# Two gate products computed while x arrives, earlier evacuation of two value tiles, and fewer buffers held back at the end of gate and up

## The chip, the cores and the metric

The kernel runs on one core of a Trainium2 chip. The metric is device time in microseconds (us) of one execution. The kernel before takes 737.2 us (median of 3 runs, 736.91 to 737.78). One more execution was profiled: it took 737.0 us, of which 735.2 us are the span that the profile shows.

A core has five engines that each run their own list of instructions strictly in order and wait for each other by semaphores: PE (matrix multiplications; PEld is its loading of weights), DVE (VectorE), ACT (ScalarE), POOL (GpSimd) and SP (which here only issues transfers). Transfers run on 16 DMA engines beside them. Matrix products go to PSUM, eight banks of 128 x 512 float32; everything else lies in SBUF.

## The reference

One encoder layer on x of 512 tokens by 1024 features, in float32:

```
proj = h @ w_in                              # queries, keys and values of two mixers
o_a = windowed_gqa_sink(qa, ka, va, sink)    # mixer A: 16 heads, 4 key heads
o_b = dilated_mixture(qb, kb, vb)            # mixer B: 12 heads in 3 groups
gates = sigmoid(h @ w_gate + b_gate)
mixed = g_a * (o_a @ w_br_a) + g_b * (o_b @ w_br_b)
h = layer_norm(ALPHA * h + mixed @ w_out)
f = (silu(h @ w_ff_gate) * (h @ w_ff_up)) @ w_ff_down
h = layer_norm(ALPHA * h + f)
```

## The kernel before

**Products.** Each float32 operand is split into two parts, a rounded high part (a copy, mostly on ACT, line 357) and the rest as a low part (a subtraction on DVE, lines 383, 406 and 469). A product of 128 x 128 weights with 512 columns of x is three matmuls (lines 496 to 498: high by high, high by low, low by high). A *unit* is 128 output features by all 1024 inputs: eight such steps of k, three matmuls each, into one PSUM bank. Its weights come in two halves of 256 KB (`half_unit`), each of which takes a landing buffer ("ws") and two buffers for its parts ("whl").

**The start.** x lies in memory as eight tiles xT of 128 features by 512 tokens (256 KB). Three units are computed along with its arrival, one each of keys, queries and values: for k = 0 to 7 the three matmuls of each (lines 1025 to 1035). Their first weight halves come in three pieces (`CUTS`: 128, 128 and 256 columns). After them follow two gate units ("g2", the first word of `ORDER`), then the second value unit ("VA"), and so on. A gate unit ends with a tanh on ACT (line 1007) that reads its PSUM bank.

**Values.** `turned_values` computes two value units, copies each from PSUM to SBUF on ACT (`evac`, printed as line 357), turns them by transposes on PE (line 681) and splits them again.

**Gate and up.** 22 times, `quad` computes 128 features of the gate and the up product by seven products of half size (12 matmuls of 256 columns each, lines 1422 to 1424), which share two PSUM banks y and xz. What stands in a bank is copied out by ACT (`keep`, line 357) before the next product may be added in the same place. The sums for the down product (`Chunk`) are worked in between; pieces for them are rounded by ACT at line 1610.

**Who sets the order.** Nothing waits by hand. The program is written as a list of operations with priorities, and a planner (`Program.run`) plays it through while the kernel is built, with a cost for every operation: at each moment a free engine takes the ready operation of highest priority whose buffers fit. What comes out is a fixed list for each engine. The priority is a point of PE's time, moved by a constant: `EV = -100` for what empties PSUM, `NORM = -150`, -130 for weights (`LOOK`); the smaller goes first. The operations at the start have absolute places (`FIRST`). `limits` says how many buffers of a class may be in use at a time, and `spare` how many of the general ones only the oldest waiting operation may take.

Of the kernel before, what the change touches and what calls it, by code (L numbers as in the profile page):

```python
# [15 lines left out]
P = 128  # L16
S = 512
# [48 lines left out]
         ("k", 1): (-996.9,), ("q", 1): (-996.7,), ("v", 1): (-996.6,),  # L66
         "x": (-999, -998.75, -997.5, -996.95, -996.8, -996.5, -996.4, -996.3)}
X_PACE = {1: None}
N_WS, N_WHL, N_ATT = 6, 12, 16


# [5 lines left out]


ORDER = """
g2 VA q1 A0 q2 q3 A1 g k1 q4 g q5 A2 g q6 g q7 A3 g2  # L80
Q00 K00 Q01 K01 V12 Q02 K02 V0 B0 Q10 K10 B1 Q11 K11 Q12 K12 B2 B3 g8
"""

# [34 lines left out]
class Program:  # L118
# [67 lines left out]
    def run(self):  # L186
# [26 lines left out]
        while n_left:  # L213
            if not times:
                self.stuck(pending)
            now = heapq.heappop(times)
            while times and times[0] <= now:
                heapq.heappop(times)
            while frees and frees[0][0] <= now:
                _, _, b = heapq.heappop(frees)  # L220
                for key in b.keys:
                    if key in self.limits:
                        self.used[key] -= 1
            progress = True
            while progress:
                progress = False
                for e in engines:
                    if free[e] > now:
                        continue
                    best = None  # L230
                    soon = now
                    for o in pending[e]:
                        if o.hold and now < o.ready <= now + HOLD and e in (DVE, ACT):
                            soon = o.ready
                        if o.ready <= now and (best is None or o.prio < best.prio) and self.fits(o):
                            if e == DVE and len(o.alts) > 1 and free[ACT] < now + BIAS:
                                continue
                            best = o
                    if best is None or soon > now and not best.hold:
                        continue  # L240
                    o = best
                    cost = dict(o.alts)[e]
                    if e == ACT and o.table not in (None, table):
                        cost, table = cost + 1.28, o.table
                    for a, _ in o.alts:
                        pending[a].remove(o)
                    for b in o.bufs:
                        if b.tile is None:
                            b.tile = b.make()
                            for key in b.keys:  # L250
                                if key in self.limits:
                                    self.used[key] += 1
                    o.fn(e)
                    o.eng = e
                    if e == SP:
                        end = now + 0.47
                        moved = max(moved, now + 0.9) + (1.5 if now < 5 else 0.92) * cost
                        o.done = moved + 0.87
                    elif o.moves:
                        end = now + cost  # L260
# [55 lines left out]
def hybrid_layer(ctx: ExitStack, tc: tile.TileContext, wpack, xT, xtok, sink, bgate,  # L316
# [6 lines left out]

    N_SLOT, HP = 85, S // 2
    pr = Program({"slot": N_SLOT, "bank": 8, **BANKS,
                  "ws": N_WS, "whl": N_WHL, "att": N_ATT, "gen": N_SLOT - 2 - N_ATT - N_WS - N_WHL,
                  "unit": UNITS, "st": 4, "x4": 4, "wf": N_WF})
    op = pr.op
    mm = nc.tensor.matmul
# [44 lines left out]
    def cp_alts(n, ps=False, cut=0.0):  # L374
        return [(ACT, act(n, ps) + cut), (DVE, dve(n, not ps) + cut)]
# [74 lines left out]

    first = {}
    for j in range(2):
        for w, u in (("k", U_KA), ("q", U_QA), ("v", U_VA)):
            first[w, j] = half_unit_by(u, j, ((0, S),) if j else CUTS, FIRST[w, j])
    got = {}
    for j in range(KD):
        st, ap = slot(F32, "xs"), FIRST["x"][j]
# [48 lines left out]
    def feat_x(ps, wu):  # L506
        for k in range(KD):
            feat_k(ps, wu, k, XM, xtok_of)
# [143 lines left out]
    def turned_values(u, nt, turn_by=0, done=None):  # L652
# [3 lines left out]
        for i in range(2):  # L656
# [13 lines left out]
                    else:  # L670
                        copy(e, d, s)

            op(cp_alts(S, True, 0.3 if turn_by else 0.1)[:2 if turn_by else 1], evac, reads=[ps], writes=[t], prio=EV)
            src.append(t)
        res = []
        for b in range(NR):
# [322 lines left out]

    away = {}  # L1000

    def gate(f, put=False):
        ps = bank("dense")
        feat_x(ps, unit(U_GATE + f))
        t = slot()
        gz[f] = t
        op([(ACT, act(S, True, 1))], lambda e: nc.scalar.activation(
            halves(t.t), back(ps.t), AF.Tanh, bias=bg.t[:, f:f + 1], scale=0.5),
           reads=[ps, bg], writes=[t], prio=EV)
        if put:  # L1010
            d = Buf("dram", None, lambda: dram.tile([P, S], F32, name=name("gz")))
            op([(SP, 0.73)], lambda e: nc.sync.dma_start(d.t, t.t), reads=[t], writes=[d], prio=EV)
            away[f] = d

    def dense_q(u, nt, kv_half):
        ps = bank("dense")
# [6 lines left out]
        return k_post(ps, nt) if nt else k_pairs(ps)  # L1023

    psk, psq, psv = bank("dense"), bank("dense"), bank("dense")
    for k in range(KD):
        for w, ps in (("k", psk), ("q", psq), ("v", psv)):
            for c in (0, S // 2) if (w, k) == ("k", 0) else (None,):
                if c is None:
                    feat_k(ps, [first[w, 0], first[w, 1]], k, XM, xtok_of, split=w == "k")  # L1030
                else:
                    op_ = feat_k(ps, [first[w, 0], first[w, 1]], k, XM, lambda k, c=c: [(xh4[0], 0, c), (xl4[0], 0, c)],
                                 n0=c, n1=c + S // 2, begins=c == 0, split=True)
                    if c == 0:
                        fill(op_)
    ka = k_near(psk, 4)
    qa = q_near(psq, 4, (0, 0))
    load(mB, maskb, prio=0)
    env = {"gate": 0, "qs": {}, "ks": {}}

    def step(w):
        if w == "VA":
# [10 lines left out]
                unit_a(g, b, qa[4 * g:4 * g + 4], ka[g], env["va"])  # L1053
        elif w[0] in "gG":
            for _ in range(int(w[1:] or 1)):
                gate((env["gate"] + 8) % 16, w[0] == "G")
                env["gate"] += 1
        elif w[0] in "QK":
            pair, g = int(w[1]), int(w[2])
# [610 lines left out]
            out[t, :, j * S + c0:j * S + c1], xt[t, j].t[:, c0:c1]), reads=[tok])  # L1670

    op([(POOL, 0.0)], lambda e: pr.limits.update(whl=4 * (N_LAST + 2)), after=[silus[-2]])
    n0 = 2 * N_PAIR * N_CHUNK
    tok_major(NFF - n0, N_LAST, lambda k: su[n0 + k], U_DOWN + n0, lg2, lb2, store, True, 1.0,
              lambda t: [chunks[c].step(n) for c, n in STEPS.get(("block", t), ())], (2, 3))
# [101 lines left out]
```

## Time and profile before

| what | us |
|---|---|
| median of 3 runs | 737.2 |
| the profiled execution | 737.0 |
| its span | 735.2 |
| PE busy in the span | 725.2 |
| DVE busy | 653.7 |
| ACT busy | 447.4 |
| POOL busy | 109.5 |

The engines' shares are averages over stages that differ. Busy PE means that a matmul is under way; since matmuls overlap, the distance from one start to the next tells whether PE lost time between them. In a row of the timeline stand the start, the duration, the engine, the line, the operation and the tiles; in brackets how long the engine was idle just before and what released it.

### The profile page before, as it was taken

The page shows a single profiled execution, that of the slowest core. Times are in us where ns is not written, and L with a number is a line of the kernel's source. Part 1 is how long each engine was busy: PE and PEld are TensorE (multiplying, and loading weights), DVE is VectorE, ACT ScalarE, POOL GpSimd, SP SyncE. Part 2 cuts the span into 40 slices and gives each one's busy share as a digit, 9 for nine tenths or more (in the row PEclk, how much of TensorE's full clock was granted, in tenths as well). Part 3 has the DMA queues.
Part 4 walks back from the last instruction along what each step waited for, and adds up shares of the span by engine and source line. Part 5 has one row for each costly group of instructions (what it writes and reads, how often), then busy time and mean ns, then how long its engine had stood idle before and what let it go on. Part 6 is the DMA issues. An engine that isn't in the chain of part 4 may idle for free.

```text
span 735.2 us, 13431 instructions
## 1 busy us (share of the span) xinstructions
PE 725.2 (99%) x4479; PEld 663.0 (90%) x4479; DVE 653.7 (89%) x1428; ACT 447.4 (61%) x1012; POOL 109.5 (15%) x273
## 2 busy tenths in 40 slices
PE   9999999999999999999999999999999999999995
PEld 6888888888888889888888999999999999999985
DVE  5879998898898999897686999799999999899977
ACT  5647687757665657774352567656666556666721
POOL 0000110000003323500010002111102111202100
PEclk9999999999999999999999999999999999999999
DMA  8824523437234765455583389776888978978402
GB/s 270 289 58 144 163 82 87 129 94 204 76 93 138 201 176 163 137 170 174 165 205 88 86 250 233 178 179 154 203 254 195 221 196 237 243 196 180 112 29 86
DMA packets 69252, 120.17 MB, mean 163 GB/s; under 512 B 8576, under 2 KB 12800, under 8 KB 69184
## 3 DMA queue, kind: packets, MB, share of 16 engines
q1 hardware_dynamic: 59040, 101.10, 44.7%
q0 software_dynamic: 9872, 18.09, 15.2%
q8 instruction: 35, 0.57, 0.3%
q14 instruction: 33, 0.27, 0.1%
q10 hardware_dynamic: 272, 0.13, 0.1%
HBM read 103.04 MB, written 2.10 MB: 143 GB/s over the span
## 4 chain that ended last, share of the span: by engine, by line
PE 94%; DMA 2%; DVE 2%; SPq 1%; ACT 1%; issue 0%; DVEq 0%; ACTq 0%
PE ps L497 12%; PE ps L496 12%; PE ps L498 12%; PE ps L1422 9%; PE ps L1424 9%; PE ps L1423 9%; PE ps L1633 4%; PE ps L1635 4%; PE ps L1634 4%; PE ps L749 3%; PE ps L1192 3%; PE ps L1193 3%; PE ps L1194 3%; PE ps L647 1%; PE ps L646 1%; PE ps L815 1%
## 5 line engine op out<-in xcount | busy, mean ns | idle before, releaser
L357 ACT ACTIVATE sl<-sl 128x512 fp32r<-128x512 f32 (+3 forms) x383 | 210.6, 582 | 62.0 <-DVE sl L1312 17.3
L1312 DVE TENSOR_TENSOR sl<-sl,sl 128x512 fp32r<-128x512 f32 (+3 forms) x294 | 167.1, 609 | 6.2 <-ACT sl L357 3.4
L357 ACT ACTIVATE sl<-ps 128x256 f32<-128x256 f32 (+5 forms) x205 | 85.8, 441 | 99.7 <-PE ps L1424 60.1
L496 PE MATMUL ps<-x,sl 128*128 128x512 f32 (+1 forms) x369 | 142.4, 386 | 0.3 <-ACT x L357 0.3
L498 PE MATMUL ps<-x,sl 128*128 128x512 f32 (+1 forms) x369 | 139.8, 379 | 0.0
L497 PE MATMUL ps<-x,sl 128*128 128x512 f32 (+1 forms) x337 | 127.9, 379 | 0.2 <-DVE x L469 0.2
L1422 PE MATMUL ps<-sl,sl 128*128 128x256 f32 x352 | 96.9, 275 | 0.6 <-ACT sl L357 0.6
L1423 PE MATMUL ps<-sl,sl 128*128 128x256 f32 x352 | 96.8, 275 | 0.0
L1424 PE MATMUL ps<-sl,sl 128*128 128x256 f32 x352 | 96.8, 275 | 0.0
L383 DVE TENSOR_TENSOR sl<-sl,sl 128x512 fp32r<-128x512 f32 x130 | 87.2, 685 | 5.1 <-ACT sl L357 4.5
L498 PEld LDWEIGHTS ps<-x,sl 128*128 128x128 f32 x369 | 69.9, 189 | 9.9 <-DVE sl L406 0.2
L496 PEld LDWEIGHTS ps<-x,sl 128*128 128x128 f32 x369 | 70.2, 190 | 8.7 <-ACT x L357 0.5
L371 POOL DMA_DIRECT2D sl<-wpack x44 | 38.5, 883 | 260.3 <-DMA sl<-wpack 72.7
L1422 PE MATMUL ps<-x,sl 128*128 128x256 f32 x264 | 72.6, 275 | 0.0
L1423 PE MATMUL ps<-x,sl 128*128 128x256 f32 x264 | 72.6, 275 | 0.0
L1424 PE MATMUL ps<-x,sl 128*128 128x256 f32 x264 | 72.6, 275 | 0.0
L497 PEld LDWEIGHTS ps<-x,sl 128*128 128x128 f32 x337 | 64.0, 190 | 7.5 <-DVE x L469 0.5
L1422 PEld LDWEIGHTS ps<-sl,sl 128*128 128x128 f32 x352 | 67.6, 192 | 0.8 <-ACT sl L357 0.7
L1423 PEld LDWEIGHTS ps<-sl,sl 128*128 128x128 f32 x352 | 67.6, 192 | 0.1
L1424 PEld LDWEIGHTS ps<-sl,sl 128*128 128x128 f32 x352 | 67.6, 192 | 0.0
L1422 PEld LDWEIGHTS ps<-x,sl 128*128 128x128 f32 x264 | 50.6, 192 | 0.4
L1423 PEld LDWEIGHTS ps<-x,sl 128*128 128x128 f32 x264 | 50.6, 192 | 0.4
(151 smaller groups left out, 1547.1 us busy)
## 6 DMA issues: line engine op xcount, KB each, us to landing
sl<-wpack SPq DMA_DIRECT2D x243, 256.0 KB, 3.7
sl<-sl SPq DMA_DIRECT2D x108, 128.0 KB, 2.3
wf<-wpack SPq DMA_DIRECT2D x51, 256.0 KB, 5.0
sl<-wpack POOLq DMA_DIRECT2D x44, 256.0 KB, 5.9
wf<-wpack POOLq DMA_DIRECT2D x24, 256.0 KB, 6.3
sl<-xtok SPq DMA_DIRECT2D x8, 256.0 KB, 3.3
out<-sl SPq DMA_DIRECT2D x7, 256.0 KB, 2.0
sl<-xT SPq DMA_DIRECT2D x6, 256.0 KB, 5.6
```

The costliest lines, as they stand in the source:

```text
L357: nc.scalar.activation(dst, src, AF.Copy)
L371: op([(POOL, 1.0)], lambda e: nc.gpsimd.dma_start(b.t, src2, accum_op=ALU.add), reads=[b], writes=[b], prio=prio, moves=1.65)
L383: op([(DVE, dve(S))], lambda e: nc.vector.tensor_tensor(l.t, src.t, f32(h.t), op=ALU.subtract), reads=[src, h], writes=[l], prio=prio, abs ...
L496: mm(o, a, x0, start=(k == 0 and begins), stop=False, skip_group_check=split)
L497: mm(o, a, x1, start=False, stop=False, skip_group_check=split)
L498: mm(o, b, x0, start=False, stop=(k == nk - 1), skip_group_check=split)
L1312: op([(DVE, dve(w))], lambda e: nc.vector.tensor_tensor(dst(), x(), y(), op=o), reads=reads, writes=writes, prio=prio)
L1422: mm(o, wh, pairs(bh[k]()), start=(first and k == 0), stop=False, skip_group_check=True)
L1423: mm(o, wh, pairs(bl[k]()), start=False, stop=False, skip_group_check=True)
L1424: mm(o, wl, pairs(bh[k]()), start=False, stop=(k == 3), skip_group_check=True)
L1633: mm(ps.t, x0, pairs(w[0].t), start=(first and m == 0), stop=False, skip_group_check=True)
L1634: mm(ps.t, x0, pairs(w[1].t), start=False, stop=False, skip_group_check=True)
```

## The change

Two gate units (features 8 and 9) are computed along with x: at each step of k there are now five products (keys, queries, values and the two gates). Their banks come from the class "s" (the two banks that later hold scores), their first halves are loaded in two pieces of 256 columns (128 KB, `ALONG_CUTS`), and "g2" goes from the head of `ORDER`. While this runs, 24 instead of 12 buffers for weight parts and two more landing buffers may be in use. The copy of the value units out of PSUM gets priority `NORM` instead of `EV`. From the third last silu on, `spare` is 8 instead of 12. The planner's costs change too: DVE's operations count 3% longer in the first 60 us, a transfer's issue counts 0.62 instead of 0.47 us between 14 and 60 us, and its data come more slowly in the first 9.5 us (before: 5 us) and 1.53 us later between 9.5 and 60 us. The unused `put` of `gate` is removed.

PE has the same number of matmuls as before. In the stretch that ran from about 365 to 664 us of the profiled span the lists of all engines are the same as before but for tiles' numbers; they differ ahead of it (the start, the two mixers, and the loads around the output product) and behind it (the last tiles of gate and up).

In the rows below each name carries the tile's number; wpack is the packed weights, xT the tiles of x.

SP's list at the start, before (sl3, sl5 and sl6 receive the weights of keys, queries and values; the row of xT with sl17 is the fourth tile of x, k = 3):

```order
L464 DMA sl8_98<-xT 128x512
L402 DMA sl3_75<-wpack 128x256
L402 DMA sl5_83<-wpack 128x256
L402 DMA sl6_85<-wpack 128x256
L464 DMA sl17_131<-xT 128x512
L402 DMA sl19_138<-wpack 128x512
L464 DMA sl21_147<-xT 128x512
```

and now (sl12 and sl15 receive the gates' weights, sl23 the fourth tile of x):

```order
L467 DMA sl8_98<-xT 128x512
L405 DMA sl12_105<-wpack 128x256
L405 DMA sl15_113<-wpack 128x256
L405 DMA sl3_75<-wpack 128x256
L405 DMA sl5_83<-wpack 128x256
L405 DMA sl6_85<-wpack 128x256
L405 DMA sl12_105<-wpack 128x256
L405 DMA sl15_113<-wpack 128x256
L467 DMA sl23_157<-xT 128x512
L405 DMA sl26_166<-wpack 128x512
L467 DMA sl27_169<-xT 128x512
```

The fourth tile of x moves back by four pieces of 128 KB; everything ahead of it stays.

ACT's list around the copies of the two value units, before (ps86 is the bank of the second one, that of the first stands two rows ahead of this piece; rows at line 1007 are the tanh of gates; 64x512 rows are parts of rotated keys and queries):

```order
L357 ACTIVATE sl73_363<-sl56_298 64x512 x2
L357 ACTIVATE sl77_374<-sl52_288 128x512
L1007 ACTIVATE sl79_382<-ps62_312,bg_67 128x512
L357 ACTIVATE sl74_364<-sl74_364 64x512
L357 ACTIVATE sl81_398<-sl53_293 128x512
L357 ACTIVATE sl84_406<-sl67_337 64x512
L357 ACTIVATE sl87_423<-sl64_320 128x512
L1007 ACTIVATE sl89_429<-ps76_369,bg_67 128x512
L357 ACTIVATE sl91_443<-sl65_326 128x512
L357 ACTIVATE sl95_462<-sl66_332 128x512
L357 ACTIVATE sl97_468<-ps86_419 128x4x64 x2
```

and now (ps20 and ps91 are the values, ps29 and ps31 the two gates):

```order
L360 ACTIVATE sl84_403<-sl67_348 128x512
L360 ACTIVATE sl86_409<-ps20_143 128x4x64 x2
L360 ACTIVATE sl88_418<-sl70_357 128x512
L360 ACTIVATE sl92_428<-sl73_366 128x512
L1011 ACTIVATE sl95_433<-ps29_180,bg_67 128x512
L1011 ACTIVATE sl96_439<-ps31_188,bg_67 128x512
L360 ACTIVATE sl100_465<-sl80_392 64x512 x2
L360 ACTIVATE sl102_472<-sl80_392 64x512
L360 ACTIVATE sl105_482<-ps91_424 128x4x64 x2
```

Both tanh now stand together, and the second value unit follows closely on the first, behind parts of the rotated keys.

ACT's list near the end of gate and up, before (ps1909 is the bank y of the last quad; its row is the copy that PE needs):

```order
L357 ACTIVATE sl1922_9044<-wf1818_8500 128x512
L357 ACTIVATE sl1924_9061<-sl1897_8881 128x512
L1610 ACTIVATE sl1927_9067<-sl1821_8519 128x256
L1610 ACTIVATE sl1928_9069<-sl1889_8851 128x256
L1610 ACTIVATE sl1929_9072<-sl1895_8874 128x256
L357 ACTIVATE sl1930_9074<-ps1909_8964 128x256
```

and now (the bank is ps1922):

```order
L360 ACTIVATE sl1930_9073<-sl1871_8777 128x512
L360 ACTIVATE sl1932_9078<-sl1901_8909 128x512
L1614 ACTIVATE sl1934_9094<-sl1894_8868 128x256
L360 ACTIVATE sl1935_9096<-sl1875_8797 128x512
L1614 ACTIVATE sl1937_9100<-sl1899_8891 128x256
L360 ACTIVATE sl1938_9103<-ps1922_9019 128x256
```

One of the three roundings at line 1610 has gone some 25 rows ahead, and a copy of a whole tile stands among them; the silu ahead of them also comes earlier.

```diff
+N_ALONG, N_WHL0 = 2, 24
+ALONG_CUTS = ((0, 256), (256, 512))
+FIRST.update({(0, 0): (-997.45, -996.97), (0, 1): (-996.65,), (1, 0): (-997.4, -996.96), (1, 1): (-996.45,)})
...
-g2 VA q1 A0 q2 q3 A1 g k1 q4 g q5 A2 g q6 g q7 A3 g2
+VA q1 A0 q2 q3 A1 g k1 q4 g q5 A2 g q6 g q7 A3 g2
...
-                    cost = dict(o.alts)[e]
+                    cost = dict(o.alts)[e] * (1.03 if e == DVE and now < 60 else 1.0)
...
-                        end = now + 0.47
-                        moved = max(moved, now + 0.9) + (1.5 if now < 5 else 0.92) * cost
-                        o.done = moved + 0.87
+                        end = now + (0.62 if 14 < now < 60 else 0.47)
+                        moved = max(moved, now + 0.9) + (1.5 if now < 9.5 else 0.92) * cost
+                        o.done = moved + (2.4 if 9.5 < now < 60 else 0.87)
...
-                  "ws": N_WS, "whl": N_WHL, "att": N_ATT, "gen": N_SLOT - 2 - N_ATT - N_WS - N_WHL,
+                  "ws": N_WS + 2, "whl": N_WHL0, "att": N_ATT, "gen": N_SLOT - 2 - N_ATT - N_WS - N_WHL,
...
-        for w, u in (("k", U_KA), ("q", U_QA), ("v", U_VA)):
-            first[w, j] = half_unit_by(u, j, ((0, S),) if j else CUTS, FIRST[w, j])
+        for w, u in (("k", U_KA), ("q", U_QA), ("v", U_VA), *((i, U_GATE + 8 + i) for i in range(N_ALONG))):
+            first[w, j] = half_unit_by(u, j, ((0, S),) if j else ALONG_CUTS if w in range(N_ALONG) else CUTS, FIRST[w, j])
...
-            op(cp_alts(S, True, 0.3 if turn_by else 0.1)[:2 if turn_by else 1], evac, reads=[ps], writes=[t], prio=EV)
+            op(cp_alts(S, True, 0.3 if turn_by else 0.1)[:2 if turn_by else 1], evac, reads=[ps], writes=[t], prio=NORM)
...
+    along = [bank("s") for _ in range(N_ALONG)]
     for k in range(KD):
-        for w, ps in (("k", psk), ("q", psq), ("v", psv)):
+        for w, ps in (("k", psk), ("q", psq), ("v", psv), *enumerate(along)):
...
+    op([(POOL, 0.0)], lambda e: pr.limits.update(whl=N_WHL, ws=N_WS), after=[pr.ops[-1]])
+    for f in range(N_ALONG):
+        gate(8 + f, along[f])
...
+    op([(POOL, 0.0)], lambda e: setattr(pr, 'spare', 8), after=[silus[-3]])
```

More of the change, by code (lines that the diff above doesn't have):

```diff
@@ L1000, in hybrid_layer, with gate @@
     away = {}
-    def gate(f, put=False):
-        ps = bank("dense")
-        feat_x(ps, unit(U_GATE + f))
+    def gate(f, ps=None):
+        if ps is None:
+            ps = bank("dense")
+            feat_x(ps, unit(U_GATE + f))
         t = slot()
@@ L1009, in gate @@
            reads=[ps, bg], writes=[t], prio=EV)
[L1010 to L1013, printed above, removed]
     def dense_q(u, nt, kv_half):
@@ L1038, in hybrid_layer @@
     load(mB, maskb, prio=0)
-    env = {"gate": 0, "qs": {}, "ks": {}}
+    env = {"gate": N_ALONG, "qs": {}, "ks": {}}
     def step(w):
@@ L1055, in step @@
             for _ in range(int(w[1:] or 1)):
-                gate((env["gate"] + 8) % 16, w[0] == "G")
+                gate((env["gate"] + 8) % 16)
                 env["gate"] += 1
```

## The prediction

> **What bounds the kernel now.** I read the page's busy times first, then who PE waited for, then the timeline at those places.
>
> ```profile
> span 735.2 us, 13431 instructions
> PE 725.2 (99%) x4479; PEld 663.0 (90%) x4479; DVE 653.7 (89%) x1428; ACT 447.4 (61%) x1012; POOL 109.5 (15%) x273
> ```
>
> PE is busy for 725.2 of 735.2 us. The change leaves the number of matmuls as it is, so it can only win what PE loses between them, and lose by new gaps. The list of waits of PE names all that it lost visibly:
>
> ```profile
> PE ps L433 <- DVE eps L483: 1.2, 1, 1.2
> PE ps L1422 <- ACT sl L357: 0.6, 1, 0.6
> PE ps L1192 <- DVE sl L1126: 0.4, 1, 0.4
> PE ps L496 <- ACT x L357: 0.3, 1, 0.3
> PE ps L497 <- DVE x L469: 0.2, 1, 0.2
> ```
>
> The first row is the very start, the last two are the arrival of a tile of x, L1422 is in gate and up, L1192 in the output product. The list counts only time with no matmul under way, so the full loss is read from the starts. PE at the tile of x:
>
> ```profile
> 10.60 0.38 PE L498 MATMUL ps<-x,sl 128*128 128x512 f32 x1
> 10.84 0.48 PE L496 MATMUL ps<-x,sl 128*128 128x512 f32 x1
> 11.16 0.38 PE L497 MATMUL ps<-x,sl 128*128 128x512 f32 x1
> 11.38 0.41 PE L498 MATMUL ps<-x,sl 128*128 128x512 f32 x1
> 12.04 0.48 PE L496 MATMUL ps<-x,sl 128*128 128x512 f32 x1 [0.25 <-ACT x L357]
> 12.76 0.48 PE L497 MATMUL ps<-x,sl 128*128 128x512 f32 x1 [0.24 <-DVE x L469]
> 13.08 0.38 PE L498 MATMUL ps<-x,sl 128*128 128x512 f32 x1
> ```
>
> Undisturbed, such matmuls start 0.216 us apart (11.16 to 11.38 shows it to the digits given). From 10.60 to 13.08 are six steps: 2.48 us instead of 1.30, so 1.18 us are lost. The place in gate and up, PE and then ACT:
>
> ```profile
> 685.12 0.28 PE L1424 MATMUL ps<-sl,sl 128*128 128x256 f32 x1
> 685.95 0.38 PE L1422 MATMUL ps<-sl,sl 128*128 128x256 f32 x1 [0.55 <-ACT sl L357]
> 686.16 0.28 PE L1423 MATMUL ps<-sl,sl 128*128 128x256 f32 x1
> ...
> 684.08 0.63 ACT L357 ACTIVATE sl<-sl 128x512 fp32r<-128x512 f32 x1 [0.26 <-DVE sl L1446]
> 684.62 1.01 ACT L1610 ACTIVATE sl<-sl 128x256 fp32r<-128x256 f32 x3
> 685.53 0.64 ACT L357 ACTIVATE sl<-ps 128x256 f32<-128x256 f32 x2
> ```
>
> Here steps are 0.11 us (686.16 to the following one, and every row before): 685.12 to 686.16 are two, 1.04 us instead of 0.22, so 0.82 us are lost. PE waits for the copy of bank y at 685.53, which stands on ACT behind one whole copy and three roundings, and ACT itself had waited for DVE until 684.08. The place in the output product:
>
> ```profile
> 376.85 0.38 PE L1194 MATMUL ps<-sl,sl 128*128 128x512 f32 x1
> 377.65 0.48 PE L1192 MATMUL ps<-sl,sl 128*128 128x512 f32 x1 [0.43 <-DVE sl L1126]
> 377.97 0.38 PE L1193 MATMUL ps<-sl,sl 128*128 128x512 f32 x1
> ```
>
> Two steps take 1.12 instead of 0.43 us: 0.69 us lost. The lists are unchanged there.
>
> **The two gate products along with x.** Removed: the 48 matmuls of two gate units behind the start; added: the same 48 within it; PE's work is equal. The gain is that PE has more to do before it needs the fourth tile of x (k = 3): 18 matmuls more (two gates, k = 0 to 2, three each), 18 x 0.216 = 3.9 us. It came there at 11.38 + 0.22 = 11.6 and would come at about 15.4 (15.5 less the 0.12 lost just before). The price is that the tile lands later, behind four pieces of 128 KB. ACT starts a rounding as soon as its data are there:
>
> ```profile
> 8.38 0.40 ACT L357 ACTIVATE sl<-sl 128x256 fp32r<-128x256 f32 x1
> 9.34 0.42 ACT L357 ACTIVATE sl<-sl 128x256 fp32r<-128x256 f32 x1 [0.56 <-DMA sl<-wpack]
> 10.37 0.42 ACT L357 ACTIVATE sl<-sl 128x256 fp32r<-128x256 f32 x1 [0.61 <-DMA sl<-wpack]
> 11.35 0.63 ACT L357 ACTIVATE x<-sl 128x512 fp32r<-128x512 f32 x1 [0.57 <-DMA sl<-xT]
> 12.03 0.63 ACT L357 ACTIVATE sl<-sl 128x512 fp32r<-128x512 f32 x1
> 12.70 0.63 ACT L357 ACTIVATE x<-sl 128x512 fp32r<-128x512 f32 x1
> ```
>
> The tile of x lands at 11.35; its low part reaches PE 1.41 us later (12.76). PE needs that 0.22 us after it begins k = 3, so there is no wait if the tile lands by 15.4 + 0.22 - 1.41 = 14.2, that is at up to 0.71 us per added piece. The rows bound a piece: 0.34 us (half of the 0.67 between whole tiles from 11.35 on) and 1.03 us (9.34 to 10.37), which means a landing between 12.7 and 15.5. I take 0.49, half of the 0.98 of the last slow tile (10.37 to 11.35), since the added pieces land just where the slow pace turns into the fast one: 13.3, with 0.9 us to spare. The gain is then the whole 1.18; at 1.03 the wait would be 1.3 us and the gain nothing.
>
> The Trainium skill ("DMA: Bandwidth & Descriptors", section "Bandwidth") speaks against cutting loads: it advises at least 1 MiB per transfer and measures 0.95 us for 64 KB against 6.15 us for 1 MB (issued from GpSimd). Between the two, 128 KB would be some 1.3 us, an estimate from that page: four pieces 5.2 us, the tile at 16.5, a wait of 2.3 us where 1.18 are lost now, and the sum below would be 737.7 instead of 735.4. The row of 1.03 us leans to its side, the 0.67 us for a whole tile right behind does not.
>
> The splitting of the four pieces is 0.42 us on ACT and about as much on DVE for each, 1.7 us. In these windows (length, then PE, PEld, DVE, ACT) both have that free, 2.9 and 2.6 us in the first two:
>
> ```profile
> 6.30:10.80 4.50, 4.50 (x23) 3.77 (x21) 2.66 (x8) 2.24 (x7) 0.00 (x0) 1.00 0.83 253
> 10.80:13.30 2.50, 2.01 (x8) 1.16 (x7) 1.71 (x3) 1.86 (x3) 0.00 (x0) 1.00 1.05 397
> 13.30:35.00 21.70, 21.70 (x102) 19.02 (x101) 19.07 (x35) 15.85 (x28) 1.66 (x8) 1.00 0.93 326
> ```
>
> The gates' first pieces stand where pieces landed by 8.38 and 9.34 before; with both roundings (9.34 + 0.42 + 0.43) they are there by 10.2, when PE, done with six products, begins the second gate. Behind the start the same megabyte of gate weights is no longer to be loaded, so I put nothing there. The gates hold the two "s" banks until their tanh. These came at 30 and 33 us, and the first scores (L646) at 44:
>
> ```profile
> L1007 ACT ACTIVATE sl<-ps,bg x2: 670/670/670, 30.2 to 33.4; 128x512 f32<-128x512 f32 x2
> L646 PE MATMUL ps<-sl,sl x80: 244/302/409, 44.0 to 290.4; 128*128 128x256 f32 x40, 128*128 128x384 f32 x32, 128*128 128x192 f32 x8
> ```
>
> Ten microseconds of cover: no cost. The two extra issues on SP cost nothing either, they go out while it only feeds a DMA that is 0.83 to 1.05 busy.
>
> **The values.** No row shows PE waiting for their copies, so that going earlier gains nothing by itself. What the new order can cost is in the second value unit. Now:
>
> ```profile
> 38.10 0.66 ACT L357 ACTIVATE sl<-ps 128x256 f32<-128x256 f32 x2 [2.96 <-PE ps L498]
> 39.85 0.60 PE L681 MATMUL ps<-ident,sl 128*128 128x128 f32 x4
> ...
> 34.71 1.90 DVE L383 TENSOR_TENSOR sl<-sl,sl 128x512 fp32r<-128x512 f32 x3
> 40.68 0.76 DVE L695 TENSOR_TENSOR sl<-ps,sl 128x256 fp32r<-128x256 f32 x2 [4.07 <-ACT sl L357]
> ```
>
> ACT had idled 2.96 us before the copy, and 1.1 us lay between its end (38.76) and the transposes. In the changed order PE ends the start at 15.4 + 75 x 0.216 = 31.6 and the second unit at 36.8; nine matmuls later, at 38.7, it wants the turned values, so the copy must begin by 38.0, as tight as before. But now it stands on ACT behind copies of rotated keys, which come from DVE, which in 13.3 to 35 us was 19.07 of 21.70 us busy and fed by a DMA that was 0.93 busy. The room is again about 1.1 us, the cost anything from 0 (the same place shows no wait) to what x cost, 1.2. Nearest is the row without a wait; I take 0.2.
>
> **The last tiles.** On ACT the needed copy now has two whole copies and two roundings ahead instead of one and three (0.53 and 0.3 us a step: 1.7 against 1.5 us). That alone would be 0.2 us worse; but PE now has three matmuls of 512 columns more ahead of the place (0.65 us), which leaves some 0.3 us of the wait, and the silu stands earlier, so that DVE's product, which released ACT at 684.08, can come sooner than that. The gain lies between 0 (DVE releases ACT 0.7 us later than now) and the full 0.82; a loss is bounded by a step of ACT, 0.3. I take the full 0.82, since 0.3 us of DVE's gain is less than one of its steps of 0.6. `spare` itself issues nothing. The planner's cost lines issue nothing either.
>
> **The sum** against the profiled execution: 737.0 - 1.18 - 0.82 + 0.2 = 735.2. The median of the runs is 0.2 higher, so 735.4. The tail stays:
>
> ```profile
> 727.50:735.20 7.70, 0.34 (x2) 0.00 (x0) 3.93 (x8) 0.29 (x1) 0.00 (x0) 0.86 0.28 103
> ```
>
> It is 7.7 us of normalising and storing with no matmul left, and its lists don't change. What is late next on PE is the 0.69 us of the output product, and the first 4.2 us.
>
> **Rivals.**
> 1. *x is late all the same.* At 1.03 us per piece, as the row at 10.37 has it, the first gain is gone: 737.2 - 0.82 + 0.2 = 736.6. For it: two of three pieces there were slow. Against: the pace is 0.67 per 256 KB from 11.35 on, where the added pieces land. The Trainium skill's figure (above) goes the same way and further. 0.20.
> 2. *The wait in the last tiles only moves.* ACT's queue ahead of the copy isn't shorter. The 0.82 stays: 736.2. 0.12.
> 3. *Slower: the second value unit.* Place: the transposes at 38.7. Price: each microsecond by which DVE's rotated keys come later than 1.1 us of room allows. With both gains made, it decides from 3.5 us of waiting (2.0 for the gains, 1.5 for the bound), so from 4.6 us of delay, a fifth of the stretch of 21.7 us. At a delay of 5 us: 737.2 - 2.0 + 3.9 = 739.1. For it: DVE 88% and DMA 93% busy there. Against: DVE's splits ended at 36.6 and it then idled 4.07 us. 0.07.
> 4. *It waits there, but less,* 0.5 to 2 us: 735.7 to 737.2, about 736.4. 0.08.
>
> **Chances.** The forecast has 0.53; its own range is 735.0 to 735.8. What a measurement of this kernel tells from no change is about 0.2%, 1.5 us: faster means under 735.7. That holds most of the forecast (0.5) and the better parts of 1, 2 and 4, where one term is only half lost or the 0.69 of the output product goes by chance (0.1): 0.60. The rest of these gives 0.32 for no difference, and 0.08 for slower. The range goes down to 734.6 (735.4 less the 0.69) and up to 736.9, above rivals 1 and 2.
>
> **What would show it.** Right: PE's waits no longer name L496 and L497 on x, and the starts run at 0.216 from 9 to 31 us; x's fourth rounding on ACT starts near 13.3; L1422 is gone from the list. Wrong: a row of L496 with "<-ACT x" near 15 to 16 us (rival 1), L1422 still there near 684 (2), L681 waiting for ACT at 38 to 41 us (3 and 4). It would also be wrong if new waits came between 60 and 365 us, where the order differs too and I see no wait now.

## The result, and the profile after

The changed kernel takes 734.48 us (median of 5 runs, 734.30 to 734.72), the kernel before 737.70 in the same session (736.91 to 738.30). The ratio is 0.9959, 95% interval 0.9944 to 0.9973: 3.2 us or 0.4% faster. The forecast of 735.4 was 0.9 us too high; the time lies just below its range's low end of 734.6. As a gain, 1.8 us were forecast (737.2 less 735.4) and 3.2 measured; 77 later runs of the kernel before have medians of 737.3 to 737.4, against which it is some 2.9. The profiled execution took 734.3 us, 2.7 less than that of before.

The page's first lines (busy time, its share and the instructions of each engine) and PE's list of waits (in all, times, longest, in us) of the changed kernel:

```profile
span 732.5 us, 13437 instructions
PE 723.8 (99%) x4479; PEld 662.8 (90%) x4479; DVE 653.6 (89%) x1433; ACT 445.8 (61%) x1011; POOL 112.2 (15%) x273
```

```profile
PE ps L436 <- DVE eps L486: 1.2, 1, 1.2
```

Of the five waits of before only the first instruction's is left. So three places became free, one of which the forecast had left as it was. "Lost in the starts" means below, as in the prediction, what the steps from one matmul to the next take beyond the undisturbed 0.216 us (0.11 for 256 columns).

**The fourth tile of x.** The timeline of ACT around its rounding, and of PE where it needs the tile:

```profile
11.04 1.13 ACT L360 ACTIVATE sl<-sl 128x256 fp32r<-128x256 f32 x3 [0.69 <-DMA sl<-wpack]
12.67 0.63 ACT L360 ACTIVATE x<-sl 128x512 fp32r<-128x512 f32 x1 [0.51 <-DMA sl<-xT]
...
15.17 0.38 PE L501 MATMUL ps<-x,sl 128*128 128x512 f32 x1
15.39 0.38 PE L499 MATMUL ps<-x,sl 128*128 128x512 f32 x1
15.60 0.38 PE L500 MATMUL ps<-x,sl 128*128 128x512 f32 x1
```

ACT idles until the tile lands, so it lands at 12.67, 1.32 us later than in the kernel before, where the forecast had 13.3 and a last moment of 14.2. PE begins the tile's products at 15.39 without a pause: 1.18 us lost before, nothing now.

**The last tiles.** ACT ahead of the copy of the bank for which PE had waited, and both kernels' windows there (length, then busy time of PE, PEld, DVE, ACT), the one of before first:

```profile
682.77 0.63 ACT L360 ACTIVATE sl<-sl 128x512 fp32r<-128x512 f32 x1 [0.85 <-DVE sl L1450]
683.30 0.40 ACT L1614 ACTIVATE sl<-sl 128x256 fp32r<-128x256 f32 x1
683.61 0.62 ACT L360 ACTIVATE sl<-sl 128x512 fp32r<-128x512 f32 x1
684.13 0.40 ACT L1614 ACTIVATE sl<-sl 128x256 fp32r<-128x256 f32 x1
684.43 0.36 ACT L360 ACTIVATE sl<-ps 128x256 f32<-128x256 f32 x1
```

```profile
684.00:687.50 3.50, 2.95 (x26) 2.76 (x25) 3.46 (x8) 3.42 (x9) 0.00 (x0) 1.00 0.43 142
```

```profile
684.00:687.50 3.50, 3.50 (x27) 3.34 (x27) 3.50 (x8) 2.69 (x8) 0.00 (x0) 1.00 0.45 143
```

DVE releases ACT at 682.77 instead of 684.08, two copies and two roundings follow, and the copy begins at 684.43 instead of 685.53. PE is busy throughout: the whole 0.82 is gained.

**The output product.** Here the forecast left 0.69 us as they were, and they are gone. The timeline ahead of it (SP, then POOL, then DVE) in the kernel before:

```profile
351.88 0.33 SPq L365 DMA_DIRECT2D sl<-xtok  x1
354.62 0.33 SPq L365 DMA_DIRECT2D sl<-wpack  x1
356.04 6.43 SPq L365 DMA_DIRECT2D sl<-xtok  x4
363.69 0.93 SPq L365 DMA_DIRECT2D sl<-wpack  x2
...
366.95 0.87 POOL L371 DMA_DIRECT2D sl<-wpack  x1 [8.43 <-DMA sl<-wpack]
...
375.10 0.69 DVE L1312 TENSOR_TENSOR sl<-sl,sl 128x512 f32<-128x512 f32 x1 [2.30 <-DMA sl<-wpack]
```

and in the changed kernel:

```profile
345.72 8.63 SPq L368 DMA_DIRECT2D sl<-wpack  x7
355.35 7.56 SPq L368 DMA_DIRECT2D sl<-xtok  x5
...
358.26 0.87 POOL L374 DMA_DIRECT2D sl<-wpack  x1 [0.65 <-DMA sl<-xtok]
...
371.61 0.69 DVE L1316 TENSOR_TENSOR sl<-sl,sl 128x512 f32<-128x512 f32 x1
```

Weights of gate and up are loaded here that POOL then completes by a second, accumulating load. In the kernel before, the first part of the second such sum stands in SP's list behind five loads of xtok; POOL's load goes out at 366.95, is there 8.1 us later, and DVE, which works its list in order, waits 2.30 us for it. Behind that row stand the branch sums that the output product needs. In the changed kernel the same weight stands ahead of all xtok loads, POOL's load goes out 8.7 us earlier (358.26) and is there by 364.6, since none of these loads took more than 6.3 us; DVE takes its row at 371.61 and does not wait. DVE's and PE's lists are the same at this place; SP's is not.

### The profile page after: what moved, and what is told of

The parts are those of the page before. It is cut to its first block, busy times and chain, and to the rows that moved or that the text cites. A ratio compares the mean times of both kernels' runs of the same rounds, so it can differ in the third digit from the quotient of the medians.

```text
span 732.5 us, 13437 instructions
## 1 busy us (share of the span) xinstructions
PE 723.8 (99%) x4479; PEld 662.8 (90%) x4479; DVE 653.6 (89%) x1433; ACT 445.8 (61%) x1011; POOL 112.2 (15%) x273
## 4 chain that ended last, share of the span: by engine, by line
PE 98%; DVE 1%; DMA 1%; ACT 0%; DVEq 0%; SPq 0%; issue 0%
PE ps L500 12%; PE ps L499 12%; PE ps L501 12%; PE ps L1428 9%; PE ps L1427 9%; PE ps L1426 9%; PE ps L1637 4%; PE ps L1638 4%; PE ps L1639 4%; PE ps L752 3%; PE ps L1196 3%; PE ps L1198 3%; PE ps L1197 3%; PE ps L650 1%; PE ps L649 1%; PE ps L818 1%
## 5 line engine op out<-in xcount | busy, mean ns | idle before, releaser
L360 ACT ACTIVATE sl<-ps 128x256 f32<-128x256 f32 (+5 forms) x211 | 88.4, 441 | 94.9 <-PE ps L1428 56.8
L501 PE MATMUL ps<-x,sl 128*128 128x512 f32 (+1 forms) x369 | 139.6, 378 | 0.0
L386 DVE TENSOR_TENSOR sl<-sl,sl 128x512 fp32r<-128x512 f32 x126 | 84.7, 685 | 7.8 <-ACT sl L360 7.0
L501 PEld LDWEIGHTS ps<-x,sl 128*128 128x128 f32 x369 | 69.7, 189 | 9.8
```

Source lines behind the costliest of these rows:

```text
L360: nc.scalar.activation(dst, src, AF.Copy)
L386: op([(DVE, dve(S))], lambda e: nc.vector.tensor_tensor(l.t, src.t, f32(h.t), op=ALU.subtract), reads=[src, h], writes=[l], prio=prio, abs ...
L501: mm(o, b, x0, start=False, stop=(k == nk - 1), skip_group_check=split)
```

## The experiments

Losses in the starts of PE in the profiled execution of each kernel, in us, and the median of its runs. The kernel before was run along with each group: 737.34 in the first (down to along1), 737.43 in the second (down to whole_cut), 737.34 in the third. The profiled execution is one of the runs, and not always a typical one: for old_costs it took 737.10, 1.15 us above the median, for tok_first5 0.61 above, for no_spare 0.37 and for spare_only 0.29. A loss in the table is that of this one execution.

| kernel | x | second value unit | output product | last tiles | median us | ratio to before |
|---|---|---|---|---|---|---|
| before | 1.18 | 0 | 0.69 | 0.82 | 737.3 to 737.7 | |
| changed | 0 | 0 | 0 | 0 | 734.48 | 0.9959 (0.9944 to 0.9973) |
| spare_only | 1.59 | 0 | 1.03 | 0 | 736.80 | 0.9992 (0.9983 to 1.0001) |
| old_costs | 0 | 1.8 | 0.91 | 0 | 735.95 | 0.9986 (0.9977 to 0.9994) |
| no_along | 1.84 | 0 | 0.57 | 0 | 737.63 | 1.0004 (0.9995 to 1.0013) |
| along1 | 0.85 | 0 | 0.61 | 0 | 735.79 | 0.9980 (0.9972 to 0.9989) |
| ln_small | 1.24 | 0 | 0 | 0.81 | 736.50 | 0.9987 (0.9978 to 0.9996) |
| tok_first5 | 0 | 0.59 | 0 | 0 | 734.41 | 0.9957 (0.9944 to 0.9971) |
| x_late | 0.46 | 0.17 | 0 | 0 | 735.50 | 0.9972 (0.9961 to 0.9983) |
| whole_cut | 0.52 (a gate's weights, not x) | 0 | 0.57 | 0 | 738.62 | 1.0020 (1.0012 to 1.0029) |
| acc_later | 1.62 | 0 | 0 | 0.81 | 736.61 | 0.9988 (0.9979 to 0.9997) |
| no_spare | 0 | 0.81 | 0 | 0.81 | 735.67 | 0.9978 (0.9969 to 0.9986) |
| dve108 | 0 | 0 | 0 | 0 | 734.66 | 0.9961 (0.9949 to 0.9974) |

### spare_only: the last part alone

In the kernel before:

```diff
+    op([(POOL, 0.0)], lambda e: setattr(pr, 'spare', 8), after=[silus[-3]])
```

> The kernel before with one line of the change alone, the one that sets spare to 8 ahead of the last three tiles. Theory of three separate places (start 1.18 us, last tiles 0.82, output product 0.69): only the last tiles change, so 0.8 us less than the kernel before (736.9 against 737.7), no row of L142x waiting for ACT near 684 us, while the rows on x and the 0.4 of the output product stay. Rival, that the gain there needs the other parts or that the wait only moves: no difference (737.7), with a wait of PE left between 682 and 687 us.

The wait at the last tiles is gone, the others stay (this kernel's list of waits):

```profile
PE ps L433 <- DVE eps L483: 1.2, 1, 1.2
PE ps L496 <- ACT x L357: 0.8, 1, 0.8
PE ps L1192 <- DVE sl L1126: 0.8, 1, 0.8
PE ps L497 <- DVE x L469: 0.2, 1, 0.2
```

The median is 0.5 us lower, with an interval from 1.3 lower to level, which holds the expected 0.8. The losses that it shares with the kernel before, at x and in the output product, are 0.4 and 0.3 us larger in this execution, at unchanged lists: so much do they move from one execution to another.

### no_spare: the change without it

In the changed kernel:

```diff
-    op([(POOL, 0.0)], lambda e: setattr(pr, 'spare', 8), after=[silus[-3]])
```

> The changed kernel without the one line that sets spare to 8 ahead of the last three tiles. Up to 680 us every list is that of the changed kernel. Theory of separate places: the wait of L142x for ACT is back, 0.8 us more than the changed kernel's 734.5: 735.3. Rival, that ACT and DVE come there at another moment since all before it is shorter: no wait, 734.5.

The wait is back with the same 0.81 us; the lists part at 663 us rather than at 680. The median is 1.2 above the changed kernel's rather than 0.8; the profiled execution also waits 0.6 us for the second value unit, at lists that are the changed kernel's (no_spare's list of waits):

```profile
PE ps L436 <- DVE eps L486: 1.2, 1, 1.2
PE ps L684 <- ACT sl L360: 0.6, 1, 0.6
PE ps L1426 <- ACT sl L360: 0.5, 1, 0.5
```

The last tiles are settled in both directions, and the room at the value unit is smaller than the one clean execution had shown.

### no_along and along1: none and one gate along with x

In the changed kernel, no_along first and then along1 (no_along also leaves the staging tiles at N_WS from the start):

```diff
-N_ALONG, N_WHL0 = 2, 24
+N_ALONG, N_WHL0 = 0, 12
...
-VA q1 A0 q2 q3 A1 g k1 q4 g q5 A2 g q6 g q7 A3 g2
+g2 VA q1 A0 q2 q3 A1 g k1 q4 g q5 A2 g q6 g q7 A3 g2
```

```diff
-N_ALONG, N_WHL0 = 2, 24
+N_ALONG, N_WHL0 = 1, 24
...
-VA q1 A0 q2 q3 A1 g k1 q4 g q5 A2 g q6 g q7 A3 g2
+g VA q1 A0 q2 q3 A1 g k1 q4 g q5 A2 g q6 g q7 A3 g2
```

> The changed kernel with no gate along with x (N_ALONG 0, the two gates back at the head of the written order, the weight limits as before); the planner's costs, the values and spare stay changed. SP's list before the xtok loads is that of the kernel before. Theory of three places: the wait for x is back (1.2 us in the starts), the output product's wait is back (0.7), only the last tiles' 0.8 is gained: 736.9. Rival, that the new costs of the planner bring the gain at the start by themselves: no wait for x, 735.7.

> The changed kernel with one gate along with x instead of two, the other at the head of the written order. PE then has 9 matmuls more before the fourth tile of x (1.94 us) and begins it at 13.5 us; the tile must land by 13.5 + 0.22 - 1.41 = 12.3. By the price seen in the changed kernel, 0.33 us a piece of 128 KB, it lands at 11.35 + 2 x 0.33 = 12.0: no wait for x. SP's list before the xtok loads is that of the kernel before, so the output product's wait is back: 2.0 us less than before, 735.7. Rival, a piece costs 1.0 us when only two stand in the queue: landing at 13.4, a wait of 1.1 us for x, 736.8.

Without the gates the wait for x is back, larger than before (1.84 us, and 0.55 more in the 20s, where L501 waits for a weight's splitting), and the output product's wait too. Instead of the expected gain of 0.8 at the last tiles the median is level, 737.63 against 737.34: that gain is there, and the larger losses at the start eat it. The new costs bring nothing by themselves. With one gate x still costs 0.85 us, where no wait was expected, since the tile landed at 13.03 and not at 12.0, nearer to the rival's 13.4 (ACT in along1's timeline):

```profile
10.59 1.09 ACT L360 ACTIVATE sl<-sl 128x256 fp32r<-128x256 f32 x3 [1.47 <-DMA sl<-wpack]
13.03 0.63 ACT L360 ACTIVATE x<-sl 128x512 fp32r<-128x512 f32 x1 [1.36 <-DMA sl<-xT]
```

With two pieces ahead of it the tile came later than in four of five executions with four pieces ahead. This is a single execution, and the landing scatters. With the same loads ahead of the tile as in the kernel before it was at 11.35, 11.70, 11.73, 11.89 and 11.91 (before, acc_later, ln_small, no_along, spare_only; mean 11.7); with those of the changed kernel at 12.15, 12.67, 12.92, 13.00 and 13.47 (tok_first5, changed, old_costs, no_spare, dve108; mean 12.8). The four pieces cost some 1.1 us on average, and the scatter of one list is as large, up to 1.3. What a single piece costs, along1 can't tell. With one gate the last moment is 12.3, only 0.6 us behind the mean landing without any piece; with two it is 14.2, behind the latest landing seen with four pieces, 13.47.

### x_late: how much room the tile has

In the changed kernel:

```diff
-         "x": (-999, -998.75, -997.5, -996.95, -996.8, -996.5, -996.4, -996.3)}
+         "x": (-999, -998.75, -997.5, -996.59, -996.58, -996.5, -996.4, -996.3)}
```

> The changed kernel with the fourth and fifth tile of x moved behind three more weight tiles of 256 KB in SP's list. At 0.67 us a tile the fourth lands at 12.65 + 2.0 = 14.65 us; PE wants it so that it must land by 14.2. Theory: a wait of 0.45 us for x near 15.4 us. The planner then also puts five roundings of rotated keys ahead of the copies of the second value unit on ACT, as in the run with the old costs (three in the changed kernel), so a wait of PE for these of 1.2 to 1.7 us near 39 us, less what PE came later. The output product keeps the order of the changed kernel and has no wait. Sum: 734.5 + 0.45 + 1.2 = 736.2. Rival: PE has more room at both places than reckoned: 734.5, no rows of x or of the values' transposes in PE's waits.

ACT and PE in this kernel:

```profile
14.84 0.64 ACT L360 ACTIVATE x<-sl 128x512 fp32r<-128x512 f32 x1
...
15.68 0.38 PE L499 MATMUL ps<-x,sl 128*128 128x512 f32 x1
16.25 0.48 PE L500 MATMUL ps<-x,sl 128*128 128x512 f32 x1 [0.19 <-DVE x L472]
```

The rounding begins at 14.84 and 0.46 us are lost for x, against 14.65 and 0.45 expected. The way from the rounding to the low part holds exactly (14.84 + 1.41 = 16.25); as PE came to the tile at 15.68 rather than 15.4, the last moment was 14.5 here. At the value unit only 0.17 us is lost, not 1.2, although five roundings stand ahead of the copies: DVE released them 0.76 us earlier (35.07) than in old_costs, and PE began the transposes 0.8 us later (38.80 against 38.02).

### old_costs: the planner's costs

In the changed kernel:

```diff
-                    cost = dict(o.alts)[e] * (1.03 if e == DVE and now < 60 else 1.0)
+                    cost = dict(o.alts)[e]
...
-                        end = now + (0.62 if 14 < now < 60 else 0.47)
-                        moved = max(moved, now + 0.9) + (1.5 if now < 9.5 else 0.92) * cost
-                        o.done = moved + (2.4 if 9.5 < now < 60 else 0.87)
+                        end = now + 0.47
+                        moved = max(moved, now + 0.9) + (1.5 if now < 5 else 0.92) * cost
+                        o.done = moved + 0.87
```

> The changed kernel with the four costs of the planner set back to those of before (gates along, values and spare kept). SP's list before the residual's eight loads is then again that of the kernel before: one weight load between the first and second xtok load and two behind the fifth, where the changed kernel has both of the first ones ahead of all eight. Theory that the output product's wait hung on this order of loads: it is back (0.4 in the list of waits, about 0.7 us in the starts), start and last tiles keep their gains, so 2.0 us less than before (735.7). Rival, that this wait goes by chance because all comes 1.2 us sooner: it is gone here too, 2.7 less (735.0). Rival, that the costs carry the gain at the start: PE waits for x or for the values before 45 us, and the time is 736.9 or more.

No wait for x: the gates alone do that. But two waits come (this kernel's list, and ACT's timeline):

```profile
PE ps L684 <- ACT sl L360: 1.5, 1, 1.5
PE ps L436 <- DVE eps L486: 1.2, 1, 1.2
PE ps L1196 <- DVE sl L1130: 0.6, 1, 0.6
```

```profile
35.83 3.23 ACT L360 ACTIVATE sl<-sl 64x512 fp32r<-64x512 f32 x5 [0.49 <-DVE sl L526]
39.07 0.66 ACT L360 ACTIVATE sl<-ps 128x256 f32<-128x256 f32 x2
```

The copies of the second value unit stand behind five roundings of rotated keys and PE waits 1.8 us for the transposes: the mechanism of the prediction's rivals 3 and 4. In the changed kernel three stand there (1.92 us from 35.62 on, the copies at 37.45). This execution is one of the slowest three of eleven; the median, 735.95, leaves room for some 0.7 us at this place rather than 1.8 (it is 1.5 above the changed kernel's, and the output product's wait, 0.7 to 0.9, is part of that; an estimate). The planner's cost lines put the roundings so; the values' new priority does not, for with the old one the changed kernel, when built, comes out the same, row for row, on every engine. The output product's wait is back with the old order of loads, though all of it comes 1 us later than in the kernel before: a later moment does not remove it. No run has the old order at an earlier moment. But in the changed kernel the rows there come only some 1.1 us earlier, while the sum is ready 7 us before DVE's row.

### dve108: one rounding instead of three

In the changed kernel:

```diff
-                    cost = dict(o.alts)[e] * (1.03 if e == DVE and now < 60 else 1.0)
+                    cost = dict(o.alts)[e] * (1.08 if e == DVE and now < 60 else 1.0)
```

> The changed kernel with the planner's factor on DVE's work ahead of 60 us at 1.08 instead of 1.03. On ACT one rounding of 64x512 stands ahead of the copies of the second value unit, where the changed kernel has three and the run with the old costs five; the load order ahead of the output product is that of the changed kernel. Theory: these roundings (0.64 us a row, released by DVE) set when the values leave PSUM, so the copies begin 1.2 us sooner than with three and PE never waits for them (it lost 0, 0.6 and 0.2 us in runs with three and five rows, 1.7 with the old costs): 734.2 to 734.5, no row of L684 in PE's waits. Rival: the copies wait for the value products of PE or the keys get late in turn: a wait elsewhere before 60 us, 735 or more.

ACT's timeline in this kernel:

```profile
37.18 0.63 ACT L360 ACTIVATE sl<-sl 64x512 fp32r<-64x512 f32 x1 [2.79 <-DVE sl L526]
37.72 0.63 ACT L360 ACTIVATE sl<-ps 128x256 f32<-128x256 f32 x2
```

The copies begin at 37.72, not 1.2 us sooner: the one rounding that is left waits longer for DVE. No wait of PE, and 734.66 against 734.48: no gain to be measured over the changed kernel. What counts at this place is DVE's release of the first rounding (35.62 in the changed kernel's profile, 37.00 in no_spare) plus the rows behind it.

### ln_small: what makes the accumulating load late

In the kernel before (the normalisation then reads the first column for all):

```diff
+    LN = 64
...
-                load(b, src[j * S:(j + 1) * S].partition_broadcast(P), after=[after], prio=-30)
+                load(b, src[j * S:j * S + n].partition_broadcast(P), after=[after], prio=-30, dst=lambda b=b: b.t[:, :n])
...
-    lg, lb = ln_vectors(ln1g, ln1b, begin)
+    lg, lb = ln_vectors(ln1g, ln1b, begin, LN)
```

> The kernel before, where the four loads of the normalisation's vectors (ln1g, ln1b) move 64 of 512 columns each and the normalisation uses the first column for all; the second set (ln2) is left as it is, by the same form of loop. So the scale and shift of the first normalisation are wrong and left out of account; every engine's list is otherwise that of the kernel before. Theory: DVE's wait of 2.3 to 2.6 us near 375 us is for POOL's second accumulating load, which went out at 366.95 and took 8.1 us because it shares the DMA engines with these four loads (1 MB). With them an eighth the size it lands in the 3.6 to 5.3 us that others take, by 372.3; DVE wants it at 372.8, so the wait of the output product is gone: 0.7 us less than before. Rival: the load goes out too late by itself (8.6 us behind the changed kernel's), the vectors are no matter: DVE's wait and 0.7 to 1.0 us on PE stay, same time as before.

POOL and DVE in this kernel's timeline:

```profile
367.38 0.87 POOL L371 DMA_DIRECT2D sl<-wpack  x1 [8.45 <-DMA sl<-wpack]
...
374.36 0.69 DVE L1321 TENSOR_TENSOR sl<-sl,sl 128x512 f32<-128x512 f32 x1 [1.17 <-DMA sl<-wpack]
```

PE's wait is gone and the median is 0.9 us lower, where 0.7 was expected; the mechanism is only half of what was expected. Without most of the vectors' traffic the load still takes 7.0 us (367.38 to 374.36), not 3.6 to 5.3, and DVE still waits 1.17 us. That is just little enough for PE. So the collision with the vectors is some 1.2 us of the delay, about half of DVE's wait. What makes the load take 7.0 us without it stays open.

### tok_first5 and acc_later: the place in SP's list, or in DVE's

In the changed kernel for tok_first5, and in the kernel before for acc_later:

```diff
-            load(xt[t, j], xtok[t, :, j * S:(j + 1) * S], after=[begin], prio=-30)
+            load(xt[t, j], xtok[t, :, j * S:(j + 1) * S], after=[begin], prio=-100 if 2 * t + j < 5 else -30)
```

```diff
-                        o.done = moved + (0.87 if e == ACT else 2.2)
+                        o.done = moved + (0.87 if e == ACT else 5 if 340 < now < 380 else 2.2)
```

> The changed kernel with the first five of the eight xtok loads given an earlier priority (100 us of lead instead of 30), so that SP issues them ahead of four weight loads, two of them the first parts of the accumulated sums. Theory that these sums' place in SP's list decides: POOL's second accumulating load goes out again at about 366 us or later, DVE waits for it near 375 and PE for DVE, 0.7 us or more: 735.2 or above, against 734.5 for the changed kernel. Rival, that only the shorter start moved this place out of a collision: no wait there, 734.5.

> The kernel before, where the planner reckons 5 us instead of 2.2 from a POOL load's last byte to its landing, for loads between 340 and 380 us alone. Up to the output product all lists stay those of the kernel before, the late weight loads included; DVE's list has the addition that waits for the second accumulated sum ten rows further down, behind the additions of the two branches on which the output product's last inputs rest. Theory, from the run with xtok first (sums as late as before, no wait of PE): the wait hung on that row's place in DVE's list; no wait of PE near 377, 0.7 to 1.0 us less than before. Rival: something else near 377 is late too and takes its place (DVE's own work is then the limit): the wait stays, same time as before.

tok_first5 refutes the first theory as it stood. POOL issues the sums as late as in the kernel before (the first at 364.89, two more from 366.46), and there is no wait of PE. Its planner, which saw the sums come late, put the second sum's row ten rows further down in DVE's list. acc_later does the same to the kernel before and changes nothing else up to there: POOL issues at 367.37, the loads take 8.3 us in the median, but the row stands behind the branch sums and PE's list of waits has no L1192:

```profile
PE ps L433 <- DVE eps L483: 1.2, 1, 1.2
PE ps L496 <- ACT x L357: 0.7, 1, 0.7
PE ps L1422 <- ACT sl L357: 0.5, 1, 0.5
PE ps L497 <- DVE x L469: 0.2, 1, 0.2
```

So three things must meet for this wait: the sum's first part late in SP's list, about 7 to 8 us for the accumulating load, and a planner that reckons 2.2 and puts DVE's row ahead of what PE needs next. Taking away any one of them (the change the first, ln_small a part of the second, acc_later the third) frees PE.

### whole_cut: fewer, larger pieces

In the changed kernel:

```diff
-ALONG_CUTS = ((0, 256), (256, 512))
-FIRST.update({(0, 0): (-997.45, -996.97), (0, 1): (-996.65,), (1, 0): (-997.4, -996.96), (1, 1): (-996.45,)})
+ALONG_CUTS = ((0, 512),)
+FIRST.update({(0, 0): (-997.45,), (0, 1): (-996.65,), (1, 0): (-997.4,), (1, 1): (-996.45,)})
```

> The changed kernel with the first half of each gate loaded as one tile of 256 KB instead of two of 128 KB (the same bytes, two issues fewer). Theory, that in a full queue the bytes set the pace: the fourth tile of x lands within 0.3 us of the changed kernel's 12.65; the first gate product has to wait for a whole tile and its roundings of 512 columns (0.63 + 0.69 us instead of 0.42 + 0.43), at most about 1 us of wait between 7 and 10 us. Rival, that small pieces cost by themselves (0.95 us for a small one, as a page of the Trainium skill, DMA: Bandwidth & Descriptors, section Bandwidth, would have it): the tile lands 1 us or more earlier. The planner also changes the order of the loads ahead of the output product to yet another one (two xtok, a weight, an xtok, a weight, four xtok, two weights), with the sums later still than in the kernel before, so a wait there of 0.7 us or more.

The fourth tile of x was there at 12.01, 0.1 to 1.5 us earlier than with the pieces cut, and SP had issued it 0.96 us earlier (7.30 against 8.26). The scatter does not let this price two issues; the Trainium skill's figure ("DMA: Bandwidth & Descriptors", section "Bandwidth"), by which the prediction had estimated 1.3 us a piece, is not borne out by any run here, for four pieces came to some 1.1 us in all. PE lost 0.52 us between 10.6 and 11.9 for the weights of the second gate, within the 1 us expected, and 0.57 in the output product, where 0.7 or more was expected. The kernel is 1.2 us slower than before for another reason, as its list of waits shows:

```profile
PE ps L818 <- DVE sl L522: 1.6, 1, 1.6
PE ps L436 <- DVE eps L486: 1.2, 1, 1.2
PE ps L499 <- DVE sl L1130: 0.3, 1, 0.3
PE ps L818 <- ACT sl L360: 0.3, 1, 0.3
PE ps L819 <- DVE sl L757: 0.2, 1, 0.2
```

L818 waits at 218 us, in the attention, at a place at which none of the other kernels waits: the edit at 8 us moved the planner's order 210 us further on. It costs 1.8 us there and 1.0 at 232.

## Why the prediction was right, and where it was not

**Right.** PE's list of waits as the place to read from; x (1.18 of 1.18 gained; x_late confirms the working of the last moment); the last tiles (0.82 of 0.82, shown by no_spare in reverse). Their sum of 2.0 us is what the profiled executions show at these places. Rival 1 (x late all the same) did not happen with two gates; with one it did in part. Rival 2 did not happen.

**The step that failed: "The lists are unchanged there", of the output product.** That was true of PE's and DVE's lists and false of SP's, which loads what DVE waits for. The 0.69 us, left standing in the sum, went with the order of loads. The prediction had them only at its low end, "by chance"; old_costs, no_along and along1, which have the order of before, all have the wait (0.57 to 0.91), while no_spare, x_late and dve108, which have the new order, have none; so it is the order, with the two conditions that ln_small and acc_later showed. The differences listed ahead of the prediction even name "the loads around the output product"; the prediction did not follow them. No line of the change aims at this place: old_costs has the gates without the costs, no_along the costs without the gates, and both come out with the old order. That the wait went is a by-product of the planner's order, and luck.

**Mis-sized: the second value unit, +0.2.** The profile of the change shows 0. Two other executions of the same list of ACT (tok_first5, no_spare) show 0.59 and 0.81, so the mean of the three is 0.5. The prediction had the right danger, copies behind rotated keys that DVE releases late, but gave the place to the values' priority, which moves no row here, and said "The planner's cost lines issue nothing either". They issue nothing, and they carry this place: without them it cost 1.8 us in the profiled execution of old_costs, and some 0.7 by the estimate from its median.

**Mis-sized: the price of a piece, 0.49.** Measured in the profile (12.67 less 11.35) / 4 = 0.33, from the means of five executions each 0.3. It changed nothing, since there was room.

**The base.** The sum stood on one execution in which x cost 1.18 us. Three more executions of the same list (spare_only, ln_small, acc_later) lost 1.59, 1.24 and 1.62 there, and the one other execution with the old lists of the output product lost 1.03 at that place. With the means (1.4, 0.9, 0.8) the gain is 3.1, close to the 2.9 to 3.2 between the medians; with the one profile 2.7.

## What to carry to other kernels

When a wait is to stay or to go, follow it back to the load: not only the list of the engine that waits, but the lists of the queues that issue what it waits for, and the order in which an engine that works in order takes its rows. A loss that a profile shows once is one draw; where it ends in a DMA, look at it in a second execution before it goes into a sum. And in a program whose order a planner makes, cost lines are edits of the program, and an edit at one place can move the order far behind it: compare the whole lists, not the places that were meant.

## What the hardware showed unexpectedly

- POOL's accumulating loads of 256 KB took 7.0 to 8.3 us in the median between 364 and 378 us in the kernel before, ln_small and acc_later, beside 3.2 to 3.5 us for SP's plain weight loads of the same size in the same stretch. With most of the vectors' traffic taken away the second one still took 7.0. In the changed kernel, which issues two of the four 7 us or more ahead of the vectors' loads, the four took 4.6 to 6.3.
- The same list of loads from the program's start put the fourth tile of x at 11.35 to 11.91 us, and that of the changed kernel at 12.15 to 13.47. Which load lands when is not settled to better than 0.6 and 1.3 us by the list alone.
